# Two heads of a pair worked off together: scores adjacent in PE's queue, products with the values interleaved chunk by chunk

## The chip, the cores and the metric

One NeuronCore of one Trainium2 chip runs the whole program in one launch. The metric is the device time of a run in microseconds. Engines are named as in the profile: PE (TensorE) multiplies matrices, PEld is its loading of stationary operands, DVE (VectorE), ACT (ScalarE) and POOL (GpSimd) work element by element, SP issues the DMAs.

## What is computed

Two layers of a diffusion-transformer block over 256 latent tokens and 256 context tokens, then one block with retention, sparse attention and a mixture of 16384 tiny experts. The change is in the attention. In the first block 8 heads of 64 dimensions attend: the latent tokens ("x") to 256 local keys with a position bias and to 256 context keys, the context tokens ("c", in the first layer only) to 256 context keys.

```python
s_loc = jnp.einsum('bjqhd,bijkhd->bhjqik', q_r, k_b) * scale + bias
s_ctx = jnp.einsum('bjqhd,bchd->bhjqc', q_r, k_ctx) * scale
p = jax.nn.softmax(jnp.concatenate([s_loc, s_ctx], axis=-1), axis=-1)
o = einsum(p_loc, v_b) + einsum(p_ctx, v_ctx)
```

In the second block 8 query heads share 2 groups of keys and values; each has a compressed branch (15 keys), a selected and a window branch (both over all causal keys at this length), mixed by gates.

## The kernel before, in words

All matrix products of the linear maps are made of three float32r products of parts (mm3, L284 to L286), the weights arriving as 512 KB units through SP's queue and being split on ACT (L238) and DVE (L242) or POOL (L240). The order on every engine is the order in which the Python code issues instructions.

Two first-block mixers (mixer, L830; layer 0 with 512 tokens, layer 1 with 256, called mixer 0 and mixer 1 here) make K and V, then work off attention *between* the matmuls of eleven further linear maps: lin (L684) calls step after every k of eight, and step (L887) advances the generator attention (L1014) every second k (512 tokens) or every fourth (256 tokens), and pops some jobs of the pooling and convolution from a list, among them pool_mix (L937), whose product goes to bank 5. An item of attention is (kind, head, query tile of 128). Mixer 0 has 32 items (16 x, 16 c), mixer 1 has 16 (x).

One step of the generator issues, in this order: the bias load of item i + 4 (prep, x items; SP and POOL), the softmax's first half of item i + 2 (soft: biased maximum on DVE L1053, its sign L1059, exponential on ACT L1060), its second half for i + 1 (scale: L1065, L1066 on DVE), then on PE the score of item i + 3 (L1043, banks 3, 4 and 7 in turn), the transposes of i (L1074, to bank 5, copied by ACT L1076) and the product with the values of i - 1 (L1088, to bank 6). A head has 64 dimensions: a score contracts 64 rows, the lower or upper half of the partitions by the head's parity; a product with the values has 64 output rows, the lower or upper half of bank 6. Every fourth item the output is split in two parts for the next linear map.

The second block's sparse attention (nsa, L1351) is built alike, with 16 items (j, group, query tile): two branches of 128 or 256 keys per item, scores at L1393, transposes at L1429 (copied at L1431), products at L1440 (compressed branch) and L1443. second_mix (L1121) advances it twice for each of eight linear maps and interleaves the generator retention (L1471). The small products L1241 and L1243 make the compressed keys and values, for two groups whose outputs are the two halves of the partitions.

## Time and profile before

| | |
|---|---|
| median of 3 runs | 2833.49 us (2833.3 to 2834.64) |
| profiled execution: span from first to last instruction | 2830.7 us |
| around the span, to the median of the runs | 2.8 us |
| PE busy | 2731.6 us, 97% |
| DVE busy | 1903.9 us, 67% |
| ACT busy | 1089.4 us, 38% |
| POOL busy | 505.6 us, 18% |
| read from HBM | 446.35 MB, 158 GB/s over the span |
| attention of mixer 0 / mixer 1 / sparse attention on PE | 469 to 589 / 1441 to 1512 / 1809 to 1892 us |

The profile gives no total time of its own for the profiled execution beside its span; the runs' median stands 2.8 us above it. A matmul's recorded duration reaches to the end of its pipeline, so consecutive matmuls overlap in the records, and what one costs in a stream is the distance from its start to the next start. An fp32 matmul stands as two passes, each with its own load of the stationary operand; a float32r one as one.

### The profile page before, as it was taken

To read this page: it belongs to the slowest core of one execution; us is meant where nothing else is said; L and a number is where in the kernel's file an instruction comes from. 1 tells how busy PE (TensorE), PEld (TensorE's weight loads), DVE (VectorE), ACT (ScalarE), POOL (GpSimd) and SP (SyncE) were. 2 spreads that over 40 slices of the span, in tenths; PEclk is the share of its full clock that TensorE was granted. 3 is DMA by queue.
4 is the path that set the end of the run, shared out by engine and by line. 5 is a ranking of instruction groups with operands and counts; after the bars stand their busy time and mean duration, and the time that the engine had idled before them with its cause. 6 is when DMAs were issued, how large, how long until landed. Compare 5 with 4: busy or idle time off the path is not lost. (4 is left out here: it accounts for less than half of the span.)

```text
span 2830.7 us, 41128 instructions
## 1 busy us (share of the span) xinstructions
PE 2731.6 (97%) x15899; PEld 2352.1 (83%) x15899; DVE 1903.9 (67%) x3580; ACT 1089.4 (38%) x1867; POOL 505.6 (18%) x284
## 2 busy tenths in 40 slices
PE   6999999999999999999999999999999988899998
PEld 4888887678888898888978999779998988888887
DVE  6777764457776565555546556675888999855555
ACT  5322234433222232222344444634443443354554
POOL 1000010020000010000121002331896555400000
PEclk9999999999999999999999999999999999999999
DMA  6555643124555535555344555424554434456664
GB/s 252 183 191 187 194 126 110 54 82 142 184 185 192 175 126 189 191 193 182 110 127 129 191 185 171 161 68 164 181 163 142 133 122 134 129 193 207 193 193 142
DMA packets 129477, 451.41 MB, mean 159 GB/s; under 512 B 16000, under 2 KB 21120, under 8 KB 127744
## 3 DMA queue, kind: packets, MB, share of 16 engines
q1 hardware_dynamic: 129280, 448.77, 49.2%
q8 instruction: 125, 2.05, 0.3%
q14 instruction: 72, 0.59, 0.1%
HBM read 446.35 MB, written 2.10 MB: 158 GB/s over the span
## 5 line engine op out<-in xcount | busy, mean ns | idle before, releaser
L284 PE MATMUL bank<-Hh,hl 128*128 128x256 f32 (+1 forms) x1968 | 663.2, 337 | 6.9 <-ACT Hh L643 5.1
L286 PE MATMUL bank<-Hh,hl 128*128 128x256 f32 (+1 forms) x1968 | 641.9, 326 | 2.7 <-POOL hl L240 2.7
L285 PE MATMUL bank<-Hl,hl 128*128 128x256 f32 (+1 forms) x1968 | 642.6, 327 | 1.7 <-DVE Hl L646 1.6
L238 ACT ACTIVATE hl<-raw 128x1024 fp32r<-128x1024 f32 (+1 forms) x401 | 411.7, 1043 | 280.3 <-DMA raw<-in_w_dram 84.7
L242 DVE TENSOR_TENSOR hl<-raw,hl 128x1024 fp32r<-128x1024 f32 (+1 forms) x316 | 381.4, 1216 | 184.6 <-ACT hl L238 183.9
L284 PEld LDWEIGHTS bank<-Hh,hl 128*128 128x128 f32 x1968 | 375.3, 191 | 51.2 <-issue 11.2
L286 PEld LDWEIGHTS bank<-Hh,hl 128*128 128x128 f32 x1968 | 375.0, 191 | 36.2 <-POOL hl L240 3.3
L285 PEld LDWEIGHTS bank<-Hl,hl 128*128 128x128 f32 x1968 | 375.4, 191 | 34.2 <-DVE Hl L646 2.7
L494 DVE SCALAR_TENSOR_TENSOR junk<-wm,cb 128x1024 bf16<-128x1024 f32 x272 | 332.0, 1221 | 12.2 <-ACT cb L500 7.7
L597 POOL TENSOR_TENSOR nacc<-nlast,nacc 128x256 f32<-128x256 f32 (+1 forms) x56 | 60.9, 1093 | 1342.6 <-issue 848.8
L240 POOL TENSOR_TENSOR hl<-raw,hl 128x1024 fp32r<-128x1024 f32 x85 | 214.6, 2532 | 194.6 <-ACT hl L238 181.9
L284 PE MATMUL bank<-G,hl 128*128 128x512 f32 (+1 forms) x673 | 229.6, 341 | 0.0
L285 PE MATMUL bank<-G,hl 128*128 128x512 f32 (+1 forms) x673 | 228.6, 340 | 0.0
L286 PE MATMUL bank<-G,hl 128*128 128x512 f32 (+1 forms) x673 | 228.5, 340 | 0.0
L310 ACT ACTIVATE G<-silu 128x512 fp32r<-128x512 f32 (+1 forms) x88 | 50.9, 579 | 414.1 <-DVE silu L783 414.1
L783 DVE TENSOR_TENSOR silu<-silu,bank 128x512 f32<-128x512 f32 (+1 forms) x88 | 54.6, 621 | 201.9 <-PE bank L286 197.1
L1807 PE MATMUL bank<-hl,Hh 128*128 128x512 f32 x768 | 179.4, 389 | 0.0
L284 PE MATMUL bank<-Hh,hm 128*128 128x512 f32 (+1 forms) x496 | 177.4, 358 | 0.0
L286 PE MATMUL bank<-Hh,hm 128*128 128x512 f32 (+1 forms) x496 | 177.1, 357 | 0.0
L285 PE MATMUL bank<-Hl,hm 128*128 128x512 f32 (+1 forms) x496 | 176.9, 357 | 0.0
L709 DVE SCALAR_TENSOR_TENSOR X<-bank,mall,X 128x256 f32<-128x256 f32 x192 | 84.5, 479 | 132.8 <-PE bank L286 132.7
L1807 PEld LDWEIGHTS bank<-hl,Hh 128*128 128x128 f32 x768 | 144.2, 188 | 29.9
(350 smaller groups left out, 5327.0 us busy)
## 6 DMA issues: line engine op xcount, KB each, us to landing
raw<-in_w_dram SPq DMA_DIRECT2D x208, 512.0 KB, 4.1
wm<-in_wmod_dram SPq DMA_DIRECT2D x128, 512.0 KB, 4.3
X<-in_wdn_dram SPq DMA_DIRECT2D x64, 512.0 KB, 3.6
raw<-in_wdn_dram SPq DMA_DIRECT2D x64, 512.0 KB, 3.6
X<-in_wup_dram SPq DMA_DIRECT2D x64, 512.0 KB, 3.6
raw<-in_wup_dram SPq DMA_DIRECT2D x64, 512.0 KB, 3.7
raw<-in_w_dram SPq DMA_DIRECT2D x64, 448.0 KB, 3.8
wm<-in_wada_dram SPq DMA_DIRECT2D x48, 512.0 KB, 4.6
```

Source lines behind the costliest of these rows:

```text
L238: nc.scalar.activation(hl[:, 0, :n], raw[:, :n], AF.Copy)
L240: nc.gpsimd.tensor_tensor(hl[:, 1, :n], raw[:, :n], hl[:, 0, :n].bitcast(F32), OP.subtract)
L242: nc.vector.tensor_tensor(hl[:, 1, :n], raw[:, :n], hl[:, 0, :n].bitcast(F32), OP.subtract)
L284: mm(o, wh, xh, start=start, stop=False)
L285: mm(o, wh, xl, start=False, stop=False)
L286: mm(o, wl, xh, start=False, stop=stop)
L310: nc.scalar.activation(dst[0], src, AF.Copy)
L494: nc.vector.scalar_tensor_tensor(junk, w, 1.0, self.cb[c], op0=OP.mult, op1=OP.mult, accum_out=o)
L597: self.nadd.tensor_tensor(acc, last, acc, OP.add)
L709: nc.vector.scalar_tensor_tensor(x, self.bank_(b, T, half), g[:, d:d + 1], x, op0=OP.mult, op1=OP.add)
L783: nc.vector.tensor_tensor(s, s, self.bank_(bb, T), OP.mult)
L1807: nc.tensor.matmul(acc[t][n], c[:, a, ts], u[:, b, n * 512:(n + 1) * 512], start=e == 0 and a + b == 0, stop=e == P - 1 and a == 1)
```

## The change

Items are ordered so that the two heads (in the sparse attention the two groups) of one query tile follow each other. score(i) issues the scores of items i and i + 1, in every second step; the sparse attention alternates the two groups within the branches. pv(i) issues the products of both items, alternating chunk by chunk, one step later than before and in the steps between. There are four softmax buffers instead of three, three instead of two for the transposed probabilities. Nothing is added to or taken from the arithmetic. Comments were removed elsewhere in the file, so that line numbers shift: L1043 becomes L1045, L1074 L1076, L1088 L1091, L1393 L1399, L1429 L1434, L1440 and L1443 L1446 and L1450.

```diff
@@ -876,8 +876,8 @@
             items = []
             for j in range(4):
                 for kind in ("x", "c") if T == 512 else ("x",):
-                    for h in (2 * j, 2 * j + 1):
-                        for qt in range(2):
+                    for qt in range(2):
+                        for h in (2 * j, 2 * j + 1):
                             items.append((kind, h, qt))
 
             attn = self.attention(l, p, C, Q, K, V, bias, items, T)
@@ -1035,19 +1035,21 @@
             bs[i] = b
 
         def score(i):
-            kind, h, qt = items[i]
-            L = 512 if kind == "x" else 256
-            pr = slice((h % 2) * 64, (h % 2) * 64 + 64)
-            q0 = (256 if kind == "c" else 0) + qt * P
-            o = self.bank[sb[i % 3]][:, :L]
-            nc.tensor.matmul(o, Q[pr, h // 2, q0:q0 + P], K[pr, h // 2, 512 - L:512], start=True, stop=True)
-            ps[i] = o
+
+            for i in (i, i + 1):
+                kind, h, qt = items[i]
+                L = 512 if kind == "x" else 256
+                pr = slice((h % 2) * 64, (h % 2) * 64 + 64)
+                q0 = (256 if kind == "c" else 0) + qt * P
+                o = self.bank[sb[i % 3]][:, :L]
+                nc.tensor.matmul(o, Q[pr, h // 2, q0:q0 + P], K[pr, h // 2, 512 - L:512], start=True, stop=True)
+                ps[i] = o
 
         def soft(i):
             kind, h, qt = items[i]
             L = 512 if kind == "x" else 256
             o, b = ps[i], bs.pop(i, None)
-            pr = p.tile([P, 512], F32, name="pr", tag="pr", bufs=3)[:, :L]
+            pr = p.tile([P, 512], F32, name="pr", tag="pr", bufs=4)[:, :L]
             st = self.sm.tile([P, 4], F32, name="sst", tag="sst", bufs=4)
             if kind == "x":
                 nc.vector.tensor_tensor_reduce(out=pr, in0=o, in1=b, op0=OP.add, op1=OP.max, scale=1.0, scalar=-3e38,
@@ -1072,22 +1074,23 @@
             pr = ps[i]
             for c in range(L // P):
                 nc.tensor.transpose(pt_b[:, c * P:(c + 1) * P], pr[:, c * P:(c + 1) * P], ident)
-            t = p.tile([P, 512], F32, name="pt", tag="pt")[:, :L]
+            t = p.tile([P, 512], F32, name="pt", tag="pt", bufs=3)[:, :L]
             nc.scalar.activation(t, pt_b[:, :L], AF.Copy)
             ps[i] = t
 
         def pv(i):
+
             kind, h, qt = items[i]
             L = 512 if kind == "x" else 256
-            t = ps.pop(i)
-            pr = slice((h % 2) * 64, (h % 2) * 64 + 64)
+            ts = [ps.pop(i), ps.pop(i + 1)]
             q4 = (i // 4) % 2
-            o = ot_b[pr, q4 * 256 + qt * P:q4 * 256 + (qt + 1) * P]
             nch = L // P
             for c in range(nch):
-                nc.tensor.matmul(o, V[:, 4 - nch + c, h * 64:(h + 1) * 64], t[:, c * P:(c + 1) * P],
-                                 start=c == 0, stop=c == nch - 1)
-            if i % 4 == 3:
+                for a in range(2):
+                    o = ot_b[a * 64:(a + 1) * 64, q4 * 256 + qt * P:q4 * 256 + (qt + 1) * P]
+                    nc.tensor.matmul(o, V[:, 4 - nch + c, (h + a) * 64:(h + a + 1) * 64], ts[a][:, c * P:(c + 1) * P],
+                                     start=c == 0, stop=c == nch - 1)
+            if i % 4 == 2:
                 src = ot_b[:, q4 * 256:(q4 + 1) * 256]
                 gh, gl = self.Gh[:, 4 + h // 2], self.Gl[:, 4 + h // 2]
                 c0 = 256 if kind == "c" else 0
@@ -1095,29 +1098,30 @@
 
         for i in range(3):
             prep(i)
-            score(i)
+        score(0)
         soft(0)
         prep(3)
         yield
         soft(1)
         scale(0)
+        score(2)
         yield
-        for i in range(n + 1):
+        for i in range(n + 2):
             if i + 4 < n:
                 prep(i + 4)
             if i + 2 < n:
                 soft(i + 2)
             if i + 1 < n:
                 scale(i + 1)
-            if i + 3 < n:
+            if i % 2 == 1 and i + 3 < n:
                 score(i + 3)
             if i < n:
                 trans(i)
-            if i >= 1:
-                pv(i - 1)
+            if i % 2 == 0 and i >= 2:
+                pv(i - 2)
             yield
 
-    # ------------------------------------------------------------ second block: retention and sparse attention
+
     def second_mix(self):
         nc, tc, I, W = self.nc, self.tc, self.I, self.W
         T = S
@@ -1134,7 +1138,7 @@
             C = {k: con[:, o:o + n] for k, (o, n) in OFF2.items() if k != "iota"}
             ident = self.C["ident"]
             NQ = Xc[:, :1024].rearrange("p (j t) -> p j t", j=4)
-            self.npts = [Xc[:, 1024:1536], Xc[:, 1536:2048]]
+            self.npts = [Xc[:, 1024:1536], Xc[:, 1536:2048], p.tile([P, 512], F32, name="npt")]
             KCV = p.tile([P, 2, T + 1], F32, name="KCV")
             KS = p.tile([P, 2, T], F32, name="KS")
             VT = p.tile([P, 2, 256], F32, name="VT")
@@ -1380,25 +1383,27 @@
             ces.append(e)
             yield
         ct = p.tile([P, 2, P], F32, name="ct")
-        items = [(j, g, qt) for j in range(4) for g in range(2) for qt in range(2)]
+        items = [(j, g, qt) for j in range(4) for qt in range(2) for g in range(2)]
         n = len(items)
         ps = {}
 
         def score(i):
-            j, g, qt = items[i]
-            gs = slice(g * 64, (g + 1) * 64)
+
+            j, _, qt = items[i]
             L = (qt + 1) * P
-            o = sc_b[i % 3].rearrange("p (b n) -> p b n", b=2)[:, :, :L]
+            for g in range(2):
+                ps[i + g] = sc_b[(i + g) % 3].rearrange("p (b n) -> p b n", b=2)[:, :, :L]
             for b in range(2):
-                nc.tensor.matmul(o[:, b], NQ[gs, j, qt * P:(qt + 1) * P], KS[gs, b, :L], start=True, stop=True)
-            ps[i] = o
+                for g in range(2):
+                    gs = slice(g * 64, (g + 1) * 64)
+                    nc.tensor.matmul(ps[i + g][:, b], NQ[gs, j, qt * P:(qt + 1) * P], KS[gs, b, :L], start=True, stop=True)
 
         def soft(i):
             j, g, qt = items[i]
             h = g * 4 + j
             L = (qt + 1) * P
             o = ps[i]
-            pr = p.tile([P, 2, S], F32, name="npr", tag="npr", bufs=3)
+            pr = p.tile([P, 2, S], F32, name="npr", tag="npr", bufs=4)
             st = self.sm.tile([P, 8], F32, name="nst", tag="nst", bufs=4)
             mask = C["caus"][:, S - L:]
             for b in range(2):
@@ -1427,45 +1432,48 @@
             for b in range(2):
                 for c in range(nb):
                     nc.tensor.transpose(pt_b[:, (b * nb + c) * P:(b * nb + c + 1) * P], pr[:, b, c * P:(c + 1) * P], ident)
-            t = self.npts[i % 2][:, :2 * nb * P]
+            t = self.npts[i % 3][:, :2 * nb * P]
             nc.scalar.activation(t, pt_b[:, :2 * nb * P], AF.Copy)
             ps[i] = t
 
         def pv(i):
-            j, g, qt = items[i]
-            t = ps.pop(i)
-            gs = slice(g * 64, (g + 1) * 64)
+
+            j, _, qt = items[i]
+            ts = [ps.pop(i), ps.pop(i + 1)]
             nb = qt + 1
-            o = ot_b[gs, (j % 2) * 256 + qt * P:(j % 2) * 256 + (qt + 1) * P]
-            nc.tensor.matmul(o, VC[:, g * 4 + j], ct[:, qt], start=True, stop=False)
+            os = [ot_b[g * 64:(g + 1) * 64, (j % 2) * 256 + qt * P:(j % 2) * 256 + (qt + 1) * P] for g in range(2)]
+            for g in range(2):
+                nc.tensor.matmul(os[g], VC[:, g * 4 + j], ct[:, qt], start=True, stop=False)
             for b in range(2):
                 for c in range(nb):
-                    nc.tensor.matmul(o, VT[:, c, b * P + g * 64:b * P + (g + 1) * 64], t[:, (b * nb + c) * P:(b * nb + c + 1) * P],
-                                     start=False, stop=b == 1 and c == nb - 1)
-            if i % 4 == 3:
+                    for g in range(2):
+                        nc.tensor.matmul(os[g], VT[:, c, b * P + g * 64:b * P + (g + 1) * 64],
+                                         ts[g][:, (b * nb + c) * P:(b * nb + c + 1) * P],
+                                         start=False, stop=b == 1 and c == nb - 1)
+            if i % 4 == 2:
                 self.split2(self.g_(S, 4 + j), ot_b[:, (j % 2) * 256:(j % 2) * 256 + 256])
 
-        for i in range(3):
-            score(i)
+        score(0)
         soft(0)
         yield
         for qt in range(2):
             nc.tensor.transpose(self.bank[2][:, qt * P:(qt + 1) * P], ces[qt].rearrange("p h n -> p (h n)"), ident)
         soft(1)
         scale(0)
+        score(2)
         nc.vector.tensor_copy(ct.rearrange("p a t -> p (a t)"), self.bank[2][:, :S])
         yield
-        for i in range(n + 1):
+        for i in range(n + 2):
             if i + 2 < n:
                 soft(i + 2)
             if i + 1 < n:
                 scale(i + 1)
-            if i + 3 < n:
+            if i % 2 == 1 and i + 3 < n:
                 score(i + 3)
             if i < n:
                 trans(i)
-            if i >= 1:
-                pv(i - 1)
+            if i % 2 == 0 and i >= 2:
+                pv(i - 2)
             yield
 
     def retention(self, p, C, RQ, RK, RV, RG):
```

How it moves PE's queue is shown at three places. The first is an odd step in mixer 1 (bank_66, bank_67 and bank_70 are the score banks 3, 4 and 7, bank_68 is bank 5, bank_69 bank 6; the rows of L284 to L286 are linear matmuls).

```order
 L285 MATMUL bank_63<-Hl,hl_77 128x256
 L286 MATMUL bank_63<-Hh,hl_77 128x256
-L1043 MATMUL bank_66<-K,Q 128x512
-L1074 MATMUL bank_68<-con_78,pr 128x128 x4
-L1088 MATMUL bank_69<-pt,V 64x128 x4
+L1045 MATMUL bank_66<-K,Q 128x512
+L1045 MATMUL bank_67<-K,Q 128x512
+L1076 MATMUL bank_68<-con_78,pr 128x128 x4
 L284 MATMUL bank_65<-Hh,hl_89 128x256
 L285 MATMUL bank_65<-Hl,hl_89 128x256
```

The score of one item has become the scores of two; the transposes stay, the product with the values is gone from this step, and linear matmuls follow the transposes.

The next step, an even one, at the following place of the queue:

```order
 L285 MATMUL bank_65<-Hl,hl_89 128x256
 L286 MATMUL bank_65<-Hh,hl_89 128x256
-L1043 MATMUL bank_67<-K,Q 128x512
-L1074 MATMUL bank_68<-con_78,pr 128x128 x4
-L1088 MATMUL bank_69<-pt,V 64x128 x4
+L1076 MATMUL bank_68<-con_78,pr 128x128 x4
+L1091 MATMUL bank_69<-pt,V 64x128 x8
 L284 MATMUL bank_65<-Hh,hl_89 128x256
 L285 MATMUL bank_65<-Hl,hl_89 128x256
```

No score stands here now. The transposes follow linear matmuls, and behind them are eight products with the values, of two items, where there were four of one.

The third place is an odd step in the sparse attention; bank_66 and bank_67 take the scores of group 0 and group 1.

```order
 L285 MATMUL bank_63<-Hl,hl_90 128x256
 L286 MATMUL bank_63<-Hh,hl_90 128x256
-L1393 MATMUL bank_66<-KS,X 128x128 x2
-L1429 MATMUL bank_68<-con_78,npr 128x128 x4
-L1440 MATMUL bank_69<-ct,Y_13007 64x128
-L1443 MATMUL bank_69<-X,VT 64x128 x2
+L1399 MATMUL bank_66<-KS,X 128x256
+L1399 MATMUL bank_67<-KS,X 128x256
+L1399 MATMUL bank_66<-KS,X 128x256
+L1399 MATMUL bank_67<-KS,X 128x256
+L1434 MATMUL bank_68<-con_78,npr 128x128 x4
 L284 MATMUL bank_63<-Hh,hl_90 128x256
```

Two matmuls of one group have become four that alternate between the groups; the products of L1440 and L1443 have moved into the next step.

## Rows read from the trace of the kernel before

**Rows 1.** Page, part 1: busy time of each engine (share of the span) and instructions.
```profile
PE 2731.6 (97%) x15899; PEld 2352.1 (83%) x15899; DVE 1903.9 (67%) x3580; ACT 1089.4 (38%) x1867; POOL 505.6 (18%) x284
```

**Rows 2.** Windows: stretch, its length, busy us (instructions) of PE, PEld, DVE, ACT, POOL; PEclk; DMA share; GB/s.
```profile
470.00:590.00 120.00, 119.78 (x558) 75.31 (x556) 56.78 (x173) 50.43 (x119) 14.86 (x18) 1.00 0.18 55
1440.00:1515.00 75.00, 73.64 (x472) 55.08 (x471) 39.85 (x111) 35.99 (x72) 24.31 (x25) 1.00 0.35 105
1808.00:1895.00 87.00, 83.55 (x519) 67.99 (x520) 57.02 (x207) 43.20 (x112) 28.84 (x15) 0.96 0.23 73
```

**Rows 3.** Timeline of PE, one step in mixer 1: start us, duration us, engine, line, operation.
```profile
1470.32 0.28 PE L286 MATMUL bank<-Hh,hl 128*128 128x256 f32 x1
1470.53 1.12 PE L1043 MATMUL bank<-K,Q 64*128 64x512 f32 x2
1471.59 0.66 PE L1074 MATMUL bank<-con,pr 128*128 128x128 f32 x4
1472.17 1.09 PE L1088 MATMUL bank<-pt,V 128*64 128x128 f32 x8
1473.19 0.39 PE L284 MATMUL bank<-Hh,hl 128*128 128x256 f32 x1
1473.41 0.28 PE L285 MATMUL bank<-Hl,hl 128*128 128x256 f32 x1
...
1474.58 0.27 PE L286 MATMUL bank<-Hh,hl 128*128 128x256 f32 x1
1474.79 0.69 PE L1043 MATMUL bank<-K,Q 64*128 64x512 f32 x1
```

**Rows 4.** Timeline of PE, three short windows at the first scores of mixer 0.
```profile
469.16 0.71 PE L1043 MATMUL bank<-K,Q 64*128 64x512 f32 x2
...
469.70 0.60 PE L1043 MATMUL bank<-K,Q 64*128 64x512 f32 x2
...
470.13 0.59 PE L1043 MATMUL bank<-K,Q 64*128 64x512 f32 x1
```

**Rows 5.** Timeline of PE, the small products L1243 of the second mixer.
```profile
1802.87 0.46 PE L1243 MATMUL bank<-wc,hid 128*64 128x64 f32 x8
1803.26 0.50 PE L1184 MATMUL bank<-hl,Hh 128*128 128x512 f32 x1
```

**Rows 6.** Timeline of PE, scores of a qt 1 item in the sparse attention.
```profile
1863.05 1.13 PE L1393 MATMUL bank<-KS,X 64*128 64x256 f32 x4
1864.11 0.44 PE L1429 MATMUL bank<-con,npr 128*128 128x128 f32 x2
```

**Rows 7.** Timeline of PE, transposes followed by linear matmuls in mixer 0.
```profile
475.12 0.66 PE L1074 MATMUL bank<-con,pr 128*128 128x128 f32 x4
...
475.85 0.39 PE L285 MATMUL bank<-Hl,hl 128*128 128x512 f32 x1
476.08 0.39 PE L286 MATMUL bank<-Hh,hl 128*128 128x512 f32 x1
```

**Rows 8.** Lines of ACT and DVE, mixer 1 (1440:1515): busy us, mean ns | idle before, releaser.
```profile
L1060 ACT ACTIVATE pr<-pr,sst 128x512 f32<-128x512 f32 x16 | 11.5, 722 | 19.4 <-DVE sst L1059 19.3 <-DVE sst L1065 0.2
L238 ACT ACTIVATE hl<-raw 128x1024 fp32r<-128x1024 f32 x10 | 10.5, 1054 | 0.0
L1076 ACT ACTIVATE pt<-bank 128x512 f32<-128x512 f32 x16 | 9.4, 590 | 13.7 <-PE bank L1074 13.7
...
L1053 DVE CUSTOM_DVE_ANT_0 pr<-bank,bias 128x512 f32<-128x512 f32 x16 | 11.0, 686 | 8.8 <-PE bank L1074 4.6 <-POOL bias L1034 4.1
L1066 DVE TENSOR_SCALAR pr<-pr,sst 128x512 f32<-128x512 f32 x16 | 9.8, 611 | 0.6
L242 DVE TENSOR_TENSOR hl<-raw,hl 128x1024 fp32r<-128x1024 f32 x7 | 8.9, 1268 | 11.8 <-ACT hl L238 11.8
```

**Rows 9.** Timeline of PE, waits for the transposes' copy: mixer 1, sparse attention.
```profile
1503.33 0.67 PE L939 MATMUL bank<-sb,pw 128*128 128x256 f32 x2 [0.92 <-ACT pt L1076]
...
1883.08 0.44 PE L1429 MATMUL bank<-con,npr 128*128 128x128 f32 x2 [1.08 <-ACT X L1431]
```

1 line of the change is left out of this document (removed).

## The prediction

> **What bounds the kernel now.** I began with the page: PE is busy for 97% of the span [rows 1], so the question is whether PE also ends the time in the stages touched. The windows view says yes: while attention runs, in mixer 0, mixer 1 and the sparse attention, PE is busy 119.78 of 120, 73.64 of 75 and 83.55 of 87 us, VectorE 47%, 53% and 66%, ScalarE 42% to 50%, the DMA engines under 0.4 [rows 2]. PE time taken out there is time gained, as long as the other two engines keep up.
>
> Then the timeline of one step [rows 3]. From one score to the next are 4.26 us; 12 linear matmuls at 0.117 (ten from 1473.41 to 1474.58) take 1.41, so a step costs 2.85. The starts split this up. Score to transposes is 1.06: two passes (every fp32 matmul stands there as two) of 512 columns and 0.20 on top; a pass is 0.43 (469.70 to 470.13, [rows 4]). Four transposes take 0.58, eight passes of values 1.02; the difference is four passes of 128 columns, so 0.11 each and 0.14 on top in both. Entering the score costs 0.09 more than the linear pace (0.21 against 0.12), and the first linear matmul behind the values 0.10 (0.22 against 0.12). Streaming is 0.86 + 0.44 + 0.88 = 2.18, the changes between kinds of matmul 0.09 + 0.20 + 0.14 + 0.14 + 0.10 = 0.67.
>
> The reader should see next that two halves of the array already work at once in this trace. The mixer opens with three scores, two on the lower 64 rows and one on the upper. Of their six passes two start together at 469.16, two at 469.70, and one by one from 470.13 [rows 4]. The half array costs no speed: the next pass follows after 0.43, as when alone. For halves by output columns there is one place, eight passes of 64 columns at L1243, both halves in turn: 0.39 us to the next matmul, of which 0.05 and 0.09 are entry and exit, so 0.25 for eight [rows 5]; one after another at half of 0.11 they would take 0.44.
>
> **The change part by part.** A pair of items here is both heads (or groups) of one query tile.
>
> Scores adjacent: per pair one of two streams is hidden. x items save 2 x 0.43 = 0.86, c items (256 columns, 0.215 a pass: (1.06 - 0.20)/4, [rows 6]) 0.43, the sparse attention 4 x 0.11 = 0.44 for qt 0 (128 columns) and 4 x 0.215 = 0.86 for qt 1 (256).
>
> Values interleaved: half of the passes go: x 8 x 0.11 = 0.88, c 0.44, qt 0 (three matmuls) 0.66, qt 1 (five) 1.10.
>
> Changes of kind: two items had 2 x 0.67; now the pair enters score and values once each. The transposes that now border on linear matmuls use the whole array, as these do: from the first of four to the second linear matmul are 0.73 us at 475.12, against 4 x 0.11 + 0.23 = 0.67 and the 0.05 to 0.14 that entering the transposes from a score costs anyway [rows 7]. Saved: 0.67. Second partners start some 0.02 late (0.71 for two where one is 0.69, [rows 3, 4]): minus 0.05.
>
> So 2.36 for an x pair, 1.49 for c, 1.72 and 2.58 for qt 0 and qt 1. Mixer 0 has 8 x and 8 c pairs: 18.9 + 11.9 = 30.8. Mixer 1: 18.9. Sparse attention: 4 x 1.72 + 4 x 2.58 = 17.2. Sum 66.9. Off this come the openings, which already overlap one score (0.86 + 0.86 + 0.44) and enter three scores at once (two entries of 0.29 in each of three stages, 1.7): **63.0 us**.
>
> Costed at nothing: the fourth pr, the third pt and npts buffer add no instruction. The bias loads keep their place in SP's queue, POOL's additions theirs. The split of attention's output comes one step later; mixer 1 uses 20 of the 22 steps its linear maps offer, mixer 0 36 of 44, so linear work still covers it.
>
> **The waits that get in.** A new one: the second score of a pair takes the bank of the softmax issued one step earlier, where it used to be three scores back. A shorter one: the transposes of the even step follow those of the odd step after 1.4 us of linear work alone, and bank 5 must be copied by ScalarE in between. What is late then is the chain at the head of a new weight unit, in durations of mixer 1 [rows 8]: split on ScalarE 1.05, on VectorE 1.27, biased maximum 0.69, exponential 0.72, copy 0.59, transposes 0.49, copy again 0.59: 5.40. Reading the accumulators, the sign of the maximum and eight hand-overs I estimate at 0.1 each, 0.8, as the entries above: 6.2. PE needs 2 x 1.41 + 3.34 = 6.16 for a pair now. There is nothing to spare, and copies of Q or the convolution stand in the same queues. Bounds: nothing, if they slip into gaps, and about 1.1 a pair, since a transpose waited 1.08 for such a copy where no score stood ahead of it [rows 9]. I take 0.5 for each of mixer 1's 8 pairs (4.0), 0.4 for each of mixer 0's 8 units, whose second pair is free of the chain (3.2), and 0.6 for the 8 pairs of the sparse attention, where VectorE is the busiest and retention hangs on it (5.0). Last, pool_mix (L939, four times) takes bank 5; it already waited 0.92 with the values ahead of it [rows 9] and now follows the transposes directly: four times 1.0 less one that was there, 3.0. Sum 15.2, bounds 0 and 35.
>
> 63.0 - 15.2 = 47.8. The profiled execution has a span of 2830.7, and 2.8 lie around it to the median of 2833.5; a difference counts alike in both. **Forecast 2786 us.**
>
> **Rivals.**
> - The waits find cover: 58 to 63 saved, 2771 to 2776. For it: ScalarE is only half busy, and the scores of a pair come earlier for VectorE. Against: the 6.2 us chain.
> - Matmuls run strictly in the order of the queue. Then the two passes of a first score go before the partner's, and only one of two overlaps: an x pair takes three score passes, not two (0.43 lost), and one pass more of values (0.11). 0.54 x 16 + 0.32 x 8 + 0.22 x 4 + 0.33 x 4 = 13.4 lost: 2799. Against: at 469.16 the upper half starts beside the first pass, three passes of the lower half overtaken [rows 4].
>   The Trainium skill's TensorE: Matmul & The Clock Gate, in Part 3 (What overlaps and what doesn't), states this rule: matmuls start and end in the order of the program. By that rule it would be 2799; the trace disagrees, with two passes inside 0.71 us at 469.16.
> - Column halves do not run at once when 128 columns stream: the 64-column case is short [rows 5]. All of the values' saving goes: 0.88 x 16 + 0.44 x 8 + 0.66 x 4 + 1.10 x 4 = 24.6; chains then wait for less (10): 63 - 24.6 - 10 = 28, 2805.
> - Neither overlap comes about, only the changes of kind are halved: 32 x 0.67 - 1.7 = 20 less 5 of waits, 2818.
> - Every pair waits 1.1 for bank 5, as at 1883.08: 35 us of waits, 28 gained, 2805.
>   TensorEngine Tiling (Array Packing) of the Trainium skill, under Performance Considerations (PSUM Bottleneck), warns that the copy out of PSUM can become the bound once PE is faster; 1883.08 shows one such wait, the stages as a whole show PE.
> - Slower than before: both steps of a pair come to hang on ScalarE's one queue, because the copy of a step stands behind the exponential of an item two ahead. The 6.2 us loop is then followed by a second one without the weight split (maximum 0.69, scaling 0.61, exponential 0.72, copy 0.59, transposes 0.49 and 0.8: 3.9), 10.1 us a pair. It decides where this passes the 8.5 us (2 x 4.26) that a pair takes today; over 32 pairs 1.6 each, 51 us: 2884. Against: VectorE and ScalarE together are busy for 47% and 42%, far from a serial loop.
>
> **How the numbers follow.** Forecast with its waits (2779 to 2793) 0.59; waits covered 0.15; strict order 0.05; no column overlap 0.06; neither 0.03; bank 5 every time 0.08; slower 0.04. The range runs from the covered case to the two at 2805: 2770 to 2806. What a measurement of this kernel can tell from no change is about 0.2%, 5.7 us; every case but the last is beyond it, so faster 0.94, slower 0.04, and 0.02 for mixtures that cancel.
>
> **What would show it.** Right: passes of two scores starting within 0.02 of each other; sixteen passes of values in about 1.1 us where eight took 1.02; no gap between transposes and linear matmuls; the three stages shorter by about 24, 12 and 11. The waits should stand before transposes (on the copy, L1078, L1436), before the second score and before L939. Wrong: a value pair of 1.9 us (columns), a score pair of 1.5 us (order), or PE idle for 1 us and more in most steps. Outside the three stages nothing should differ by more than 1 us.

## The result, and the profile after

The changed kernel runs in 2798.72 us (median of 4, 2793.06 to 2801.68), the kernel before, run beside it, in 2833.39 (median of 4, 2829.94 to 2834.64): a ratio of 0.9873, 95% interval 0.986 to 0.9886, so 1.3% faster. The profiled execution took 2793.06 us, its span is 2791.3, 39.4 less than before. The forecast was 2786 in a range of 2770 to 2806: the direction held and the range held the time, 12.7 us above the forecast.

The page's first part and the windows over the three stages (the columns of [rows 2]), from the first score to the end of the last products:

```profile
PE 2678.0 (96%) x15899; PEld 2323.3 (83%) x15899; DVE 1905.2 (68%) x3580; ACT 1087.7 (39%) x1867; POOL 506.5 (18%) x284
```

```profile
471.00:566.00 95.00, 92.79 (x563) 63.05 (x560) 57.43 (x174) 49.69 (x119) 15.20 (x18) 1.00 0.22 69
1415.00:1480.00 65.00, 59.21 (x468) 47.47 (x468) 40.98 (x111) 35.03 (x72) 25.25 (x25) 0.97 0.38 115
1774.00:1856.00 82.00, 70.02 (x516) 58.04 (x517) 57.34 (x205) 42.60 (x112) 28.65 (x14) 0.94 0.25 78
```

PE is busy for 53.6 us less over the span, yet only 39.4 were gained. The other 14.2 turned into idle time of PE: in mixer 1 it is busy 59.21 of 65 us where it was 73.64 of 75, in the sparse attention 70.02 of 82 where it was 83.55 of 87 [rows 2]. In mixer 0 it stays near full. The granted clock falls too, from 1.00 to 0.97 in mixer 1 and from 0.96 to 0.94 in the sparse attention; in mixer 0 it stays at 1.00.

From one paired score to the next in mixer 1, two steps, are 6.12 us; the prediction said 6.16, before it was 8.5:

```profile
1430.00 1.13 PE L1045 MATMUL bank<-K,Q 64*128 64x512 f32 x4
...
1436.12 1.13 PE L1045 MATMUL bank<-K,Q 64*128 64x512 f32 x4
```

One even and one odd step of mixer 1 on PE (an odd one near the end, which has no score), which answer to [rows 3]:

```profile
1460.20 0.60 PE L1076 MATMUL bank<-con,pr 128*128 128x128 f32 x4
1460.73 1.09 PE L1091 MATMUL bank<-pt,V 128*64 128x128 f32 x16
1461.76 0.39 PE L284 MATMUL bank<-Hh,hl 128*128 128x256 f32 x1
...
1464.20 0.66 PE L1076 MATMUL bank<-con,pr 128*128 128x128 f32 x4 [0.78 <-ACT pt L1078]
1467.99 1.19 PE L939 MATMUL bank<-sb,pw 128*128 128x256 f32 x2 [3.13 <-ACT pt L1078]
1468.62 0.78 PE L284 MATMUL bank<-Hh,hl 128*128 128x256 f32 x1
1469.20 0.41 PE L285 MATMUL bank<-Hl,hl 128*128 128x256 f32 x1
```

Sixteen passes of values take 1.03 us to the next matmul, as eight did before (1.02): the halves by output columns run at once. What follows is the price: transposes wait 0.78, the pooling's product L939 waits 3.13 where it waited 0.92 [rows 9]. Behind that wait the linear matmuls start 0.21 apart and not 0.12: the granted clock is at the lower of its two levels, 1.2 GHz, from 1468.0 to 1471.4. By these two distances about half of the time that PE is busy at the lower level is lost; the estimates of the clock's cost below go by that.

Two scores of a pair on PE, the first of mixer 0 [rows 4] and a qt 1 pair of the sparse attention [rows 6]:

```profile
470.37 1.13 PE L1045 MATMUL bank<-K,Q 64*128 64x512 f32 x4
471.43 0.50 PE L284 MATMUL bank<-Hh,hl 128*128 128x512 f32 x1
```

```profile
1797.01 1.14 PE L1399 MATMUL bank<-KS,X 64*128 64x256 f32 x8
1798.08 0.66 PE L1434 MATMUL bank<-con,npr 128*128 128x128 f32 x4
1798.49 0.37 PE L284 MATMUL bank<-Hh,hl 128*128 128x256 f32 x1
```

Four passes of 512 columns take 1.06, eight of 256 take 1.07, each as long as half as many before. The first linear matmul starts within 0.41 of the transposes' first pass, without a gap.

PE's waits by what they waited for, in mixer 1 and, except for one more of 0.7, in the sparse attention (us in total, times, longest):

```profile
PE bank L939 <- ACT pt L1078: 4.4, 2, 3.1
PE bank L1076 <- ACT pt L1078: 1.2, 2, 0.8
```

```profile
PE bank L1434 <- ACT npt L1436: 2.2, 1, 2.2
PE bank L1434 <- ACT X L1436: 2.1, 1, 2.1
PE bank L1434 <- DVE mv L1507: 1.5, 1, 1.5
PE bank L1487 <- DVE RK L1167: 1.5, 1, 1.5
PE bank L284 <- ACT RV L1320: 1.2, 1, 1.2
PE bank L1399 <- DVE ce L1373: 1.2, 1, 1.2
PE bank L1163 <- ACT rsrc L1159: 1.2, 3, 0.5
PE bank L284 <- DVE ry L1516: 1.1, 1, 1.1
```

The same view of before sums to 0.2, 1.3 and 5.0 us; now it is 2.2 (for the copies of Q, 1.4, and of pt, 0.8), 5.6 and, with one more wait of 0.7, 12.7. The wait for RV is new too: the first of the eight linear maps beside the sparse attention takes a bank whose copy is not done.

The engines' durations in mixer 1, as in [rows 8]:

```profile
L1062 ACT ACTIVATE pr<-pr,sst 128x512 f32<-128x512 f32 x16 | 11.5, 722 | 19.6 <-DVE sst L1061 18.7 <-DVE sst L1067 0.6
...
L1078 ACT ACTIVATE pt<-bank 128x512 f32<-128x512 f32 x16 | 9.3, 584 | 6.0 <-PE bank L1076 6.0
```

```profile
L1068 DVE TENSOR_SCALAR pr<-pr,sst 128x512 f32<-128x512 f32 x16 | 11.6, 723 | 0.6
```

The scaling L1068 takes 723 ns on the mean where it took 611; the other operations of the chain differ from before by 50 ns at most. Most of the sixteen scalings take 488. The two longest, 1.59 and 2.32 us, start while GpSimd is in a split of weights (L240), and each ends 0.29 us behind it (at 1426.42 and 1431.81); before there was one such, of 1.80. ACT's idle time ahead of the copy, spent waiting for PE, falls from 13.7 to 6.0; its 19.6 ahead of the exponential, waiting for DVE, stays.

What the 3.13 us wait waited for is read from all engines' timeline of those microseconds, DVE and ACT rows:

```profile
1460.80 1.23 DVE L242 TENSOR_TENSOR hl<-raw,hl 128x1024 fp32r<-128x1024 f32 x1 [1.72 <-PE bank L1076]
...
1462.86 0.72 ACT L1062 ACTIVATE pr<-pr,sst 128x512 f32<-128x512 f32 x1 [2.09 <-DVE sst L1061]
...
1464.46 0.42 DVE L311 TENSOR_TENSOR G<-bank,G 128x256 fp32r<-128x256 f32 x1 [1.05 <-ACT G L310]
1464.80 0.41 DVE L928 TENSOR_TENSOR sb<-sa,conb 64x256 f32<-64x256 f32 x1
...
1465.68 0.69 DVE L1055 CUSTOM_DVE_ANT_0 pr<-bank,bias 128x512 f32<-128x512 f32 x1
...
1466.60 0.72 ACT L1062 ACTIVATE pr<-pr,sst 128x512 f32<-128x512 f32 x1 [2.17 <-DVE sst L1061]
...
1467.32 0.57 ACT L1078 ACTIVATE pt<-bank 128x512 f32<-128x512 f32 x1
```

The transposes end at 1464.86, but their copy L1078 starts at 1467.32: it stands in ACT's queue behind the exponential L1062 of an item two ahead, which waits 2.17 for DVE, where three operations of other work stand ahead of the biased maximum L1055. The first of them, L311, itself came 1.05 late: it waited for ACT's part of the same split of the output (L310), which stands behind the exponential of 1462.86, and that one had waited 2.09 for a maximum issued behind DVE's split of weights L242. So the two queues wait for each other in turn, with L242 in the loop; in between ACT is idle, and late by its order.

### The profile page after: what moved, and what is told of

Read it like the earlier page. It is cut to its first block, busy times and chain, and to the rows that moved or that the text cites. A ratio compares the mean times of both kernels' runs of the same rounds, so it can differ in the third digit from the quotient of the medians.

```text
span 2791.3 us, 41127 instructions
## 1 busy us (share of the span) xinstructions
PE 2678.0 (96%) x15899; PEld 2323.3 (83%) x15899; DVE 1905.2 (68%) x3580; ACT 1087.7 (39%) x1867; POOL 506.5 (18%) x284
## 5 line engine op out<-in xcount | busy, mean ns | idle before, releaser
L284 PE MATMUL bank<-Hh,hl 128*128 128x256 f32 (+1 forms) x1968 | 663.0, 337 | 9.3 <-ACT Hh L643 5.1
L286 PE MATMUL bank<-Hh,hl 128*128 128x256 f32 (+1 forms) x1968 | 641.5, 326 | 2.7 <-POOL hl L240 2.7
L242 DVE TENSOR_TENSOR hl<-raw,hl 128x1024 fp32r<-128x1024 f32 (+1 forms) x316 | 383.2, 1222 | 178.4 <-ACT hl L238 175.9
L284 PEld LDWEIGHTS bank<-Hh,hl 128*128 128x128 f32 x1968 | 375.2, 191 | 50.5 <-issue 7.9
L286 PEld LDWEIGHTS bank<-Hh,hl 128*128 128x128 f32 x1968 | 374.8, 190 | 36.1 <-POOL hl L240 3.3
L240 POOL TENSOR_TENSOR hl<-raw,hl 128x1024 fp32r<-128x1024 f32 x85 | 214.1, 2527 | 188.6 <-ACT hl L238 164.3
L284 PE MATMUL bank<-G,hl 128*128 128x512 f32 (+1 forms) x673 | 229.5, 341 | 0.0
L286 PE MATMUL bank<-G,hl 128*128 128x512 f32 (+1 forms) x673 | 228.3, 339 | 0.0
L310 ACT ACTIVATE G<-silu 128x512 fp32r<-128x512 f32 (+1 forms) x88 | 50.9, 579 | 414.1 <-DVE silu L783 414.1
L284 PE MATMUL bank<-Hh,hm 128*128 128x512 f32 (+1 forms) x496 | 177.8, 358 | 0.0
L286 PE MATMUL bank<-Hh,hm 128*128 128x512 f32 (+1 forms) x496 | 177.4, 358 | 0.0
```

Source lines behind the costliest of these rows:

```text
L240: nc.gpsimd.tensor_tensor(hl[:, 1, :n], raw[:, :n], hl[:, 0, :n].bitcast(F32), OP.subtract)
L242: nc.vector.tensor_tensor(hl[:, 1, :n], raw[:, :n], hl[:, 0, :n].bitcast(F32), OP.subtract)
L284: mm(o, wh, xh, start=start, stop=False)
L286: mm(o, wl, xh, start=False, stop=stop)
```

## The experiments

The stages are compared by the start of the same linear matmul (the n-th of L284) in both traces; in before the marks are 468.4 and 591.4, 1438.1 and 1515.1, 1700.1 and 1960.0. The first four columns are differences to before in us; "rest" is all that lies outside, up to the end of the span. The last two columns are, between the same marks, how long PE waited and how long the granted clock stood at the lower level:

| kernel | mixer 0 | mixer 1 | sparse attention | rest | mixer 1: waits / lower clock | sparse attention: waits / lower clock |
|---|---|---|---|---|---|---|
| before | | | | | 1.8 / 0 | 18.8 / 27.3 |
| after | -26.5 | -9.7 | -5.0 | +1.8 | 6.1 / 3.4 | 26.7 / 34.1 |
| scores only | -13.7 | -6.4 | -5.3 | -1.1 | 2.4 / 0 | 20.2 / 23.9 |
| values only | -14.6 | -4.8 | -2.4 | +3.3 | 4.7 / 3.4 | 23.4 / 30.7 |
| not interleaved | -23.4 | -8.6 | -3.0 | +5.0 | 5.0 / 0 | 25.0 / 30.7 |
| copy first | -24.8 | -9.9 | -9.0 | -0.7 | 6.1 / 3.4 | 27.2 / 20.5 |
| pooling product later | -26.2 | -10.3 | -5.4 | +1.7 | 6.1 / 3.4 | 27.5 / 30.7 |
| split on VectorE | -26.1 | -7.9 | 0.0 | +7.6 | 6.1 / 10.2 | 28.9 / 41.0 |
| copy first (sparse), product later | -26.3 | -10.6 | -7.7 | +5.6 | 5.7 / 3.4 | 28.1 / 23.9 |
| these and split on VectorE | -26.5 | -10.3 | -3.7 | +1.0 | 6.1 / 3.4 | 28.0 / 34.1 |
| rotation later | -26.5 | -10.8 | -3.0 | +8.3 | 5.7 / 3.4 | 29.0 / 34.1 |
| free bank | -26.2 | -10.7 | -9.5 | +5.4 | 5.7 / 3.4 | 26.2 / 23.9 |
| split on GpSimd | -26.3 | -15.4 | -8.9 | +5.0 | 2.8 / 0 | 27.1 / 20.5 |
| free bank, split on GpSimd | -26.3 | -15.0 | -9.4 | +7.0 | 3.2 / 0 | 25.9 / 23.9 |

Mixer 0, which in after and the last eight kernels differs in no more than the place of the pooling product, comes out at 26.1 to 26.5 in all nine; its clock never falls. The other stages repeat less well, and the granted clock goes with it. Mixer 1, untouched by the split on VectorE, gains 7.9 there and 9.7 in after, with the same waits but 10.2 us at the lower level instead of 3.4. In the sparse attention the lower level stands for 20.5 to 41.0 us; a difference of 10 us there is worth some 5 where PE is busy. The rest, mostly in the expert block at the end, moves by 9 us in the same way: behind the last mark the lower level stands for 28.5 us with the rotation later and for 9.2 in after.

Whole times move with it too. The four executions of the kernel with the split on VectorE took 2790.24 and 2793.06 us at a granted clock of 0.991, 2805.23 and 2805.95 at 0.985; those of after 2793.06 at 0.989 to 2801.68 at 0.987. Only one execution of each kernel was traced, so a stage is read here with its waits and its clock beside it.

**Scores alone, values alone.** The first undoes the interleaved products (pv of one item, every step), the second the paired scores (score of one item, every step); the lines that decide:

```diff
-            if i % 2 == 0 and i >= 2:
-                pv(i - 2)
+            if i >= 1:
+                pv(i - 1)
```

```diff
-            for i in (i, i + 1):
+            for i in (i,):
...
-            if i % 2 == 1 and i + 3 < n:
+            if i + 3 < n:
```

> The pairs' scores stay adjacent, in every second step; the products with the values go back to one item in every step, as before the change. Theory A (tiles of the array overlap, each part adds its streams and its changes of kind): the step without a score saves 0.09 + 0.20 + 0.10 of changes, so 0.86 + 0.39 - 0.05 = 1.20 us per x pair, 0.77 per c pair, 0.78 and 1.20 for qt 0 and qt 1; 33.3 in all, less 3.9 for the openings, less some 5 of waits: 24 us under the kernel before, about 2809. Mixer 0 some 13, mixer 1 some 7, sparse attention some 5 us shorter than before. Rival B (nearly all of the gain is the overlap of the products): under 12 us gained. Rival C (what was lost of the sum is lost by scores that take the bank of the softmax one step back): gain under 15 and PE waits in front of second scores.

> One score in every step as before the change; the products with the values of both items interleaved, in every second step. Theory A: the step without products saves 0.14 + 0.10 of changes, so 0.88 + 0.24 - 0.05 = 1.07 us per x pair, 0.63 per c pair, 0.85 and 1.29 for qt 0 and qt 1: 30.8 in all, less some 5 of waits: 26 us under the kernel before, about 2808. Together with the scores-only kernel more than the change itself gains, if the loss is in waits that appear once PE is fast enough; as much as the change gains, if the two parts simply add. Rival B (nearly all of the gain is here): 32 or more.

Measured: 2816.15 us (2805.88 to 2822.23), ratio 0.9938 [0.9917, 0.996], and 2814.02, 0.9933 [0.9915, 0.9952]. By their medians both gain less than was expected, 17 and 19 us where 24 and 26 were said; the stages of the scores alone are those of theory A (13.7, 6.4 and 5.3, where 13, 7 and 5 were said), those of the values alone sum to 21.8. Each half is worth some 14 us in mixer 0, and both together (28.3) nearly what they bring at once (26.5). In the sparse attention the scores alone bring as much as both (5.3 against 5.0): what the values add there is lost, to waits (26.7 us against 20.2) and to the clock (34.1 us at the lower level against 23.9).

**Products not interleaved.** All chunks of one head, then all of the other (the sparse attention likewise).

```diff
-            for c in range(nch):
-                for a in range(2):
+            for a in range(2):
+                for c in range(nch):
```

> The change, but the products of a pair are issued item after item, not chunk by chunk. Theory A (each half of the array has a queue of its own that holds some four passes, as 1799.8 to 1800.3 shows for L1362, where the second half starts when the first half's fifth pass of eight starts): second items start when four passes of the first are left, an x pair takes 12 passes instead of 8 (0.44 us), c pairs lose nothing, qt 0 and qt 1 0.22 and 0.65: 10.5 us in all, part of it hidden behind waits, so 5 to 10 us slower than the change. Rival B (only neighbours overlap): 15 for 8 passes in an x pair, 7 for 4 in a c pair, 21 us slower. Rival C (the queue looks far ahead, interleaving is needless): as the change.

Measured: 2802.26, 0.9888 [0.9868, 0.9908]; 3.1, 1.1 and 2.0 us less gained in the three stages, 6.2 in all, within theory A's 5 to 10; the medians are 3.5 apart. The values of one pair on PE:

```profile
1430.34 1.58 PE L1091 MATMUL bank<-pt,V 128*64 128x128 f32 x16
1431.85 0.39 PE L284 MATMUL bank<-Hh,hl 128*128 128x256 f32 x1
```

1.51 us to the next matmul: 0.48 more than interleaved, and 0.5 less than two times 1.02. The trace's starts tell how: the second head's first pass, ninth in the queue, starts at 1430.835 together with the first head's fifth (1430.829), and its next three beside the sixth to eighth; the last four run alone. So twelve passes' time, as theory A said. The ninth pass went ahead of three passes that stood before it (sixth to eighth), and did not start while more of them were left. This is why the interleaving matters, and why pairing alone already has half of what the values save.

**Copy ahead of the exponential.** In both generators trans (and its copy on ACT) is issued ahead of soft and scale.

```diff
-            if i + 2 < n:
-                soft(i + 2)
-            if i + 1 < n:
-                scale(i + 1)
             if i % 2 == 1 and i + 3 < n:
                 score(i + 3)
             if i < n:
                 trans(i)
+            if i + 2 < n:
+                soft(i + 2)
+            if i + 1 < n:
+                scale(i + 1)
```

> The change, with score and transposes issued ahead of the softmax of later items in a step, so that on ScalarE the copy of the transposes stands ahead of the exponential of the item two ahead. PE's order is that of the change. Theory A (PE's waits of 0.6 to 2.3 us in front of transposes and of L939 come from the copy standing behind an exponential that waits for a late VectorE): those waits go, mixer 1 some 4 us shorter, sparse attention some 5, about 2789. Rival B (VectorE itself is the bound there): the waits only change their name, transposes then wait for the scaling, within 2 us of the change. Rival C: exponentials now wait for transposes and the chain gets longer: slower.

Measured: 2790.46, 0.9856 [0.9832, 0.9879]. In the sparse attention 4.0 us are gained over after, in mixer 0 1.7 lost, in mixer 1 nothing changes. Transposes no longer wait for the copy but for the scaling before them (sparse attention, then mixer 1):

```profile
PE bank L1434 <- DVE npr L1425: 3.8, 3, 1.5
```

```profile
PE bank L939 <- DVE sb L932: 4.7, 2, 3.0
PE bank L1076 <- DVE pr L1068: 1.0, 2, 0.7
```

With ACT's order out of the way, the same waits are DVE's: L939 has its bank but not its input. In mixer 1 VectorE is late too. Rival B, that the waits only change their name, holds in both stages: in the sparse attention PE waits for 27.2 us where it was 26.7. What differs there is the clock, 20.5 us at the lower level where it was 34.1. In five of the seven kernels with this edit it is 20.5 to 23.9, in the kernels that pair both and lack it 30.7 to 41.0; so the edit may keep the clock up by where it puts the waits, but that isn't shown.

**The pooling product later.** pool_mix is taken from the list one step later.

```diff
                 todo.extend([lambda: mean(slice(0, 64), 1), lambda: mean(slice(64, P), 2), rest,
-                             lambda: pool_mix(pc, sums[pc][2][:, :, 8:S + 8])])
+                             *[lambda: None] * (pops - 1), lambda: pool_mix(pc, sums[pc][2][:, :, 8:S + 8])])
```

> The change, with the product of the pooling (L939) in mixer 1 issued one step after the subtraction it reads, not in the same step. Theory A: PE's two longest waits of mixer 1 (1.45 and 3.30 us in front of L939) come from a product that asks for data VectorE has only just been told to make, behind a softmax; a step later both are there: mixer 1 4 us shorter than the change, the rest alike. Rival B (the copy of the transposes from bank 5 is what is waited for, wherever the product stands): the waits stay within 1 us, no gain.

Measured: 2792.83, 0.9854 [0.9832, 0.9876]; mixer 1 gains 0.6 us, within the scatter. The waits of 4.4 and 1.2 have become 2.9 before L939 and 2.3 before the transposes, both for the copy L1078. Where the product stands decides who waits, hardly how long, as rival B said.

**The split of the weights of the retention's queries and keys on VectorE** instead of GpSimd, eight units: GpSimd and VectorE might stand in each other's way.

```diff
-... (label[0] == "win2f" and label[1] > 7 or label[0] == "win2r" ...
+... (label[0] == "win2r" ...
```

> The change, with the splits of the retention's query and key weights (eight units in the sparse attention) on VectorE instead of GpSimd. Theory A (GpSimd's split holds VectorE: L1167 takes 2.15 us beside it and 0.42 without; that lateness is what transposes wait for): L1167 takes 0.42 everywhere, the waits of 2.3, 1.7 and 2.3 us before transposes shrink to under 1, sparse attention 3 us shorter. Rival B (VectorE is simply full there: 57 us of work in some 80): eight more splits of 1.23 us make 10 us more of work for it, transposes wait longer, 4 us slower or more.

Measured: 2799.15, 0.9866 [0.9835, 0.9898]; the median of after is 2798.72. In the trace the sparse attention gains nothing over before, 5.0 less than after. Between the marks VectorE has no more to do (170.05 us, 170.19 in after): eight splits came, and three of the five long turns described below went. Two of the eight turns still take 2.15 us, not the 0.42 that theory A said.

```profile
1664.70:1924.60 259.90, 231.01 (x1701) 210.89 (x1699) 170.05 (x403) 123.58 (x240) 53.74 (x38) 0.92 0.43 139
```

```profile
1787.44 1.04 ACT L238 ACTIVATE hl<-raw 128x1024 fp32r<-128x1024 f32 x1
...
1788.51 1.23 DVE L242 TENSOR_TENSOR hl<-raw,hl 128x1024 fp32r<-128x1024 f32 x1 [4.10 <-ACT hl L238]
```

VectorE waits 4.10 for ACT's half of the split, and the softmax L1410 stands behind it. But PE's waits grow by only 2.2 us (28.9 against 26.7), those before transposes not at all (5.7 against 5.8); the larger part of the 5.0 goes with the clock (41.0 us at the lower level against 34.1), and the traced execution was the longest of its four. A cost of the edit isn't shown. On top of the next kernel the same edit has 4.0 us less in the sparse attention as well:

> The three edits together: copy first in the sparse attention, pooling's product later, splits of the retention's weights on VectorE. By theory A of the split's run 3 us under the kernel with two of them, about 2787; by its rival B 4 us or more over it.

Measured: 2792.93, 0.986 [0.9829, 0.989]; 3.7 us gained in the sparse attention instead of 7.7. The waits are equal (28.0 and 28.1), the lower clock is not (34.1 and 23.9), and the medians are alike (2793.74 without the edit). So neither theory A's 3 us of gain nor B's 4 of loss is shown.

**Copy first in the sparse attention alone, product later.**

> The change with both helps that the theory of waits names: the copy ahead of the exponential in the sparse attention alone (where it shortened the stage by 4 us; in mixer 0 it cost 1.7), and the pooling's product one step later in mixer 1 (4 us). If the waits are separate: 8 us under the change, about 2789 to 2791, mixer 0 as in the change. If what is late is VectorE in both: 4 or less, as the wait turns up at the next instruction.

Measured: 2793.74, 0.9859 [0.9839, 0.9879], 5 us under after where 8 were expected of separate waits; stages 26.3, 10.6 and 7.7, the sum of what the edits did alone to within 2 us. PE waits for no less than in after (5.7 and 28.1 us), so the waits did turn up again. The rotation, the free bank and the split on GpSimd are edits of this kernel.

**The rotation later.** On VectorE one operation of the rotary turn stands out in the sparse attention, before (L1163) as after (L1167); min, median and max in ns:

```profile
L1163 DVE TENSOR_TENSOR RQ<-rsrc,rtmp x4: 2130/2142/2159, 1841.3 to 1894.3; 128x256 f32<-128x256 f32 x4
```

```profile
L1167 DVE TENSOR_TENSOR RQ<-rsrc,rtmp x4: 2142/2150/2162, 1803.9 to 1855.6; 128x256 f32<-128x256 f32 x4
L1167 DVE TENSOR_TENSOR RK<-rsrc,rtmp x3: 424/425/2135, 1814.2 to 1849.9; 128x256 f32<-128x256 f32 x3
```

The same operation takes 0.42 or 2.15 us. In each of the five turns of after that take 2.15 (of eight; the last starts behind the window) and the four of before, GpSimd is in a split of 2.4 when it starts, and it ends 0.3 us behind that; in the others no split is under way. The first of after:

```profile
1803.33 2.43 POOL L240 TENSOR_TENSOR hl<-raw,hl 128x1024 fp32r<-128x1024 f32 x1 [4.08 <-ACT hl L238]
...
1803.45 0.42 DVE L1166 TENSOR_TENSOR rtmp<-bank,con 128x256 f32<-128x256 f32 x1
...
1803.90 2.15 DVE L1167 TENSOR_TENSOR RQ<-rsrc,rtmp 128x256 f32<-128x256 f32 x1
```

L1166, which has a bank among its inputs, is not held. This agrees with the Trainium skill's SBUF — State Buffer, section "SBUF: two separate sides": a VectorE operation with both inputs in buffers and a GpSimd operation that reads buffers exclude each other for the whole instruction, and who starts first goes on. The run moves the turn from the second to the fifth k of a map, where GpSimd has finished, and retention's next step by one k.

```diff
-                    if k == 1:
-                        flush()
                     if k == 3 or k == 7:
                         next(nsa, None)
-                    if k == 5 and n > 1:
+                    if k == 4:
+                        flush()
+                    if k == 6 and n > 1:
                         next(ret)
```

> On top of the kernel with copy first and the pooling's product later: in the sparse attention the rotation of the retention's queries and keys (L1164 to L1167 on VectorE) is issued behind the even step's softmax, after the fifth k of a unit instead of the second, retention's step one k later. Theory A (GpSimd's split holds L1167, and with it the softmax queued behind): GpSimd is done by then, L1167 takes 0.43 us, the waits of 1.7, 1.0 and 1.6 us in front of transposes go, some 1 us comes back where retention's score wants the rotated keys at once: stage 2 to 3 us shorter. Rival B (VectorE's amount of work is the bound): the stage's length stays within 1 us.

Measured: 2796.04, 0.9857 [0.9836, 0.9878].

```profile
L1167 DVE TENSOR_TENSOR RQ<-rsrc,rtmp x4: 424/425/426, 1804.2 to 1852.9; 128x256 f32<-128x256 f32 x4
```

```profile
PE bank L1487 <- DVE RK L1167: 3.8, 3, 1.9
PE bank L1525 <- DVE rtmp L1166: 3.8, 2, 2.2
...
PE bank L1434 <- DVE npr L1425: 0.4, 2, 0.2
```

In this window the collision is gone and the transposes' waits with it, 3.8 to 0.4 us; the eighth turn, behind it, meets a split again and takes 2.12. But retention now waits 7.6 us for the later turn, and 3.0 more behind the window. So a turn ahead of the softmax was what the transposes waited for; since the edit moves the turn as well as ending the collision, the run does not tell the two apart. All waits together are 0.9 us longer than without the edit (29.0 against 28.1). The stage is 4.7 worse, but most of that goes with the clock (34.1 us at the lower level against 23.9): two of the four executions took 2791.3 and 2791.6 us at a granted clock of 0.990, no more than the kernel without the edit, two 2800.5 and 2801.3 at 0.986, and the traced one is of these. That this way costs more than it saves isn't shown.

**A free bank for the first map.** The map takes bank 2 and not bank 0, so that it need not wait for the copy of RV.

```diff
-                o = self.bank[n % 2][:, :T]
+                o = self.bank[n % 2 if n else 2][:, :T]
...
```

> On top of the same kernel: the first of the eight linear maps in the sparse attention writes bank 2, not bank 0, which ScalarE still copies (L1320). Theory: the wait of 2.49 us at the start of that map goes, and the half clock that follows it; stage 2.5 to 4 us shorter. Rival: the wait turns up at the next transposes or at the second map's bank 1, under 1 us gained.

Measured: 2790.76, 0.9847 [0.983, 0.9863]. The wait of 2.3 is gone; the waits before L1163 grow from 1.6 to 2.5. In all PE waits 1.9 us less (26.2 against 28.1) with the same time at the lower level (23.9), and the stage gains 1.8: what it gains is the wait taken away, between the theory's 2.5 to 4 and the rival's 1.

**The split of mixer 1's weights on GpSimd** for all but five of the units, where three were there before.

```diff
-... label[:2] == ("winf", 1) and label[2] in (0, 4, 11) ...
+... label[:2] == ("winf", 1) and label[2] not in (8, 12, 13, 14, 15) ...
```

> On top of the same kernel: in mixer 1 the splits of all weights that are used between the attention's steps are on GpSimd (seven or eight more units of 2.4 us). Theory A (mixer 1 is bound by the chain through VectorE's 1.27 us split in front of the softmax): the chain of 6.2 us loses 1.27, and mixer 1 becomes 3 to 5 us shorter. Rival B (VectorE's scaling L1068 is held by GpSimd's splits, and GpSimd's bias additions come later): the waits stay or grow, mixer 1 up to 5 us longer.

Measured: 2786.26 (2781.72 to 2786.82), 0.9822 [0.9806, 0.9838], the fastest kernel of the study. Mixer 1 gains 15.4 us instead of 10.6, as theory A said. L242 runs twice there, not seven times, and PE's waits are halved:

```profile
PE bank L1045 <- DVE sst L1055: 1.2, 1, 1.2
PE bank L1076 <- ACT pt L1078: 0.8, 1, 0.8
...
PE bank L939 <- ACT pt L1078: 0.3, 1, 0.3
```

The chain through VectorE's split was what mixer 1 waited for, and with it gone the copy behind the exponential costs 1.1 us where it cost 5.2. Of the 4.8 us gained 2.9 are waits (2.8 left of 5.7); the clock no longer falls in the stage, where it stood at the lower level for 3.4 us, which is worth some 1.7. VectorE pays: its scalings L1068 take 960 ns on the mean and not 723 (485 at best, 2331 at worst), as five of the sixteen now meet a split, and it waits 26.1 us for biases that GpSimd adds later. That is rival B's mechanism, but it does not make VectorE late for PE.

**Both of these.**

> The kernel with the split on GpSimd, and the first map of the second mixer moved to a free bank as well. Theory A (each wait that is taken away is PE time gained, since the wait stands alone in its stage): mixer 1 as with the split alone, 15 us shorter than before; the wait of about 2.5 us for the copy of the retention's values (RV) is gone, and the sparse attention is 9.5 to 10.5 us shorter than before, 1 to 2 more than the 8.9 of the split alone; the time about 1.5 us less than the split alone, 2784 to 2785. Rival B (the sparse attention is held by VectorE's chain, so a wait taken away comes back at the next place where PE meets that chain): sparse attention 8.5 to 9 shorter, the time at 2786 as with the split alone, and a new wait for VectorE or for the accumulators of the maps ahead of the sparse attention.

Measured: 2791.42 (2788.15 to 2799.18), 0.9855 [0.9828, 0.9881]. Stages 15.0 and 9.4, against 15.4 and 8.9 without the bank. The RV wait is gone, waits for rsrc have grown to 2.5 us in all; some 0.5 us are left of 2.3. PE waits 1.2 us less in all, and the clock stands 3.4 us longer at the lower level. The whole times' intervals overlap, so the two are not told apart; neither theory's time is confirmed by it.

## Why the prediction was right, and where it was off

- **Overlap, both kinds: right.** Partners of a value pair start 0.006 to 0.007 us apart, pairs 0.109, and 16 passes take 1.03 where the prediction said about 1.1. Of 0.88 + 0.86 an x pair saves all, and the pair of mixer 1 took 6.12 us where 6.16 were said. The scores-only and values-only kernels show each part by itself.
- **Order of the queue: right.** The rival of strict order (2799) lies near the median, yet is not the cause, and that the median fits it is luck: by it a score pair takes three passes, 1.5 us, and it took 1.06; and without interleaving two heads would take all but one of their sixteen passes one by one, some 1.8 us, and took 1.51. The rule of the Trainium skill's TensorE: Matmul & The Clock Gate, Part 3, that matmuls start and end in program order, is not borne out: a pass that is ninth in the queue started beside the fifth.
- **Mixer 0: right.** About 24 was said, 26.5 came. Gross it is 30.8 less its openings of 1.44 (0.86 and two entries of 0.29), 29.4; so 2.9 were lost, of which 2.0 are new waits in the view. The 3.2 for its units was a little too much, and its share of the pooling term was nothing: its two products L939 stand behind the last step, at 565.6 and 577.6, and did not wait.
- **Mixer 1: mechanism right, size off.** Of 17.5 gross (18.9 - 1.44) 9.7 came, 12 was said: 7.8 lost where the step "0.5 for each of mixer 1's 8 pairs (4.0)" and two pooling products (1.5) give 5.5. The view has 4.3 us of new waits (5.6 less 1.3); the 3.4 us at the lower clock are another 1.7, which the sum did not have at all; 1.8 stay open. The chain was named rightly: "split on ScalarE 1.05, on VectorE 1.27, biased maximum 0.69, exponential 0.72, copy 0.59", a few hundredths beyond PE's pair; moving the split away took most of its waits.
- **Sparse attention: the term that was mis-sized.** 16.2 gross (17.2 less 0.44 and 0.58), 5.0 came, 11 was said. "0.6 for the 8 pairs of the sparse attention, where VectorE is the busiest and retention hangs on it (5.0)" should have been 11.2. Of it 7.7 are new waits in the view and 2.5 the clock (PE is busy for 28.0 us at the lower level between the marks, where it was 23.0). The waits are no fixed toll on each pair, as the step put it, but single places, eleven waits of 0.3 to 2.2: the copy behind the exponential (4.3), retention's and its turn's, RV. What it overlooked stood in the trace before: an operation of 2.14 us on VectorE, five times its length, at every second map. While PE was the slower side no wait of PE's named it. Of the edits that took such places away one by one, the free bank gave 1.9 us of waits back, copy first none.
- **The pooling product: right in place, wrong as a separate cost.** It waited 4.4 us in mixer 1 (3.0 was said for all four), but placed later the same time was waited elsewhere: it belongs to the chain, and a term of its own was no cause of its own.
- **The sum: the waits right, partly by luck, the clock missing.** Over the span PE's idle time grew by 14.2 us where 15.2 of waits were said; too much for mixer 0 and too little for the sparse attention made up for each other. What the sum put at nothing, without a word, is the clock: PE is busy at the lower level for 45.8 us and not 34.3, which costs some 5.8. The gross saving is then 53.6 + 5.8 = 59.4 (an estimate) where 63.0 was said. 59.4 less 14.2 and 5.8 is the 39.4 of the traced execution.
- **"Outside the three stages nothing should differ by more than 1 us": not quite.** The span's start differs by 1.2 us, and 1.0 is given back behind mixer 1. In medians the gain is 34.7, in the profiled executions 39.4, against the 47.8 forecast: the profiled execution is the shortest of its four, and the others, up to 8.6 us longer, ran at a granted clock of 0.987 to 0.988 and not 0.989. Where in the span they lost it isn't known, as they were not traced.
- **Other rivals.** Column overlap failing, neither overlap and the serial loop are excluded by the starts and the steps. A wait in every pair: mixer 0 has two in 16 pairs. Covered waits: no, 14.2 us of them are new.

Left open: how much of the sparse attention's remaining 7 us is retention's own chain on VectorE. Only its rotation was moved, and that added a wait of its own. A kernel without GpSimd's split and without ScalarE's half ahead of the softmax wasn't tried. It is also open why one execution of a kernel is granted less of the clock than another.

## What to carry to other kernels

Two products that use half of the array each are worth pairing, with their passes alternating in the queue; the saving can be worked out beforehand from pass lengths, over the span to a tenth here (63.0 said, 59.4 by estimate). What is left of it is set by the chain of the slower engines: work out its length per pair against PE's new length, look at where a copy that PE needs stands behind work it doesn't need, and at single operations that last several times their usual length, since cover that hid them goes when PE gets faster. Move the longest link of the chain to an engine that is idle (here the split to GpSimd, 4.8 us) before moving the one that waits. And before you credit an edit with a few us in a stage, compare PE's waits and the granted clock there: four of the edits here moved the sparse attention by 4 to 5 us, while PE's waits in it changed by 0.1 to 2.2.

## What the runs showed of the hardware that was not expected

- PE started a pass for the other half of the array ahead of three passes before it in the queue, and not of all eight: the ninth pass of sixteen started with the fifth, before the sixth to eighth.
- A VectorE operation with both inputs in buffers that meets a GpSimd split of 2.4 us took 2.15 us and not 0.425, to just behind the split's end; one that reads a bank (L1166) took its usual 0.42. Moved out of GpSimd's way, the seven in the window took 0.425; the eighth met a split and took 2.12. A scaling from buffer to buffer (L1068) is held in the same way, 2.32 us and not 0.488. A GpSimd operation on 128x2 elements (L1509) that stands over the start of a turn at 1859.77 did not hold it (0.425). Such rows were in the trace of before, and the prediction did not use them.
- A wait of PE's can cost a second time: behind the 3.13 us wait the granted clock was at 1.2 GHz from 1468.0 to 1471.4, and the linear matmuls ran 0.21 apart where they had run 0.12. Behind mixer 0's waits of 1.4 and 0.8 us it stayed at 2.4 GHz.
- The same kernel is granted different clocks: four executions with the split on VectorE had 0.991, 0.991, 0.985 and 0.985, and took 2790.24, 2793.06, 2805.23 and 2805.95 us.
